# The last block of each MLP: another order of products, a scaled sum in DRAM, and weight forms made ahead

## The chip, the cores and the metric

The kernel runs on one core of a Trainium2 chip. The metric is the time of one execution on the device in microseconds (us). The engines are TensorE (PE, matrix products, with PEld for its weight loads), VectorE (DVE), ScalarE (ACT), GpSimd (POOL) and SyncE (SP). SP and POOL do little but issue transfers here: SP the plain loads, POOL the transfers that copy or add inside DRAM.

## The reference

A trunk of two layers on 512 tokens of width 1024, in float32:

```python
def hybrid_layer(x, ...):
    h = rmsnorm(x, g_mix)
    z = h @ w_in                       # q, k, v of attention and of retention, gates
    ya = sliding_window_sink_attention(aq, ak, av, sinks) @ w_a
    yb = (retention(rq, rk, rv), normed and gated) @ w_b
    x = x + (sigmoid(ga) * ya + sigmoid(gb) * yb) @ w_out
    h2 = rmsnorm(x, g_mlp)
    return x + jnp.square(jax.nn.relu(h2 @ w_up)) @ w_down     # d_ff = 4096

def reference(x, ...):
    for l in range(2):
        x = hybrid_layer(x, ...)
    return rmsnorm(x, g_final)
```

The change lies in the last line of the layer, the MLP, and in what stands around its end: the first projection of the next layer, and the final norm.

## The kernel before, in words

Every product of float32 matrices is made of three matrix products of rounded parts (hi times hi, hi times lo, lo times hi: lines 322 to 324, in `products`). A weight unit of 128x1024 numbers is loaded to a `raw` tile (five buffers), ACT rounds it to `hi` (line 276), and DVE subtracts to get `lo` (line 277); four `hi` and four `lo` buffers exist. `unit` hands out the next unit and has the splitting kept three units ahead and the loading four more. The list of units, and with it the order of loads and splits, is written out by hand in `unit_order`.

The MLP runs in eight blocks of 512 of the 4096 hidden columns. A block makes 512 hidden columns (two calls of `pair`; in block 0 plain products of `w_up`) and then multiplies them into the sum of the MLP in `down(e)`. Both steps use a scheme for a 2x2 split of the matrices that needs seven products instead of eight. Its seven weight forms are blocks of the weights and sums of blocks. In `down`, the seven are units 0 to 6 of the block: w11, a sum from DRAM, w11 plus that sum, w12, another sum from DRAM, the full sum, and w21. Units 2 and 5 are added on DVE from raw tiles that are kept for it (`add_block`, line 258). The sums from DRAM are made earlier by POOL: `sum_steps` is a generator, and each second call of `pace` during the attention and retention part of a layer issues its next step.

Each product of `down` leaves an accumulator in PSUM (a, b or c, two banks each, one per `m`). The four quarters of the output are (i, j): i is the half of the 1024 columns, j the half of the 512 tokens. In blocks 0 to 6 (class `Adding`) ACT copies each finished accumulator to a temporary (lines 1177 and 1182) and POOL issues a transfer that adds it to `y` in DRAM (line 1187). There are seven temporaries, shared with `pair`.

In block 7 (class `Ending`) SP loads the four quarters of `y` into tiles called `big` (line 1199; six buffers, shared with the hidden columns and the forms). ACT multiplies the loaded sum by a factor per token (line 1210), since the norm before the MLP was left out of its input: the square of that norm's scale comes out as a factor on the sum. In layer 1 the residual x is put into `y` too, divided by the factor (`turn_x`). DVE then adds each accumulator times the factor (lines 1228 and 1229). In layer 0 the quarters are turned back by PE (`turn`, line 1252) and added to x by DVE (line 1258); `scaled_input` makes the operands of the next layer from x (lines 332 and 333, tiles xh and xl), and the next layer's first projection (`group`) begins. One quarter is turned after that projection's first unit (`carry`). In layer 1 the quarters get the final norm: ACT sums squares (line 1234), DVE multiplies by the gain (line 1235), ACT takes the root (line 1239), and ACT scales the eight pieces (line 1243), which SP and ACT store (line 1244).

A planner of the framework orders the instructions of each engine: it runs the program on a timing model, and an engine takes the first instruction in program order that the model has ready. The order on the chip is fixed by that; an engine, and the queue of SP or POOL, then waits at an instruction whose inputs are late even if a later one could run.

## Time and profile before

| | |
|---|---|
| median of 3 runs | 1505.0 us (1504.91 to 1506.18) |
| the profiled execution | 1507.86 us, its span 1505.9 us |
| PE busy | 1472.5 us, 98% |
| DVE busy | 1067.4 us, 71% |
| ACT busy | 945.4 us, 63% |
| POOL busy | 228.8 us, 15% |
| mean granted TensorE clock | 0.994 |
| moved | 284.68 MB, mean 189 GB/s |

All positions are microseconds from the start of the span. Layer 0 ends, and layer 1 begins, near 740. The MLP of layer 0 runs from about 430 to 740, that of layer 1 from about 1160 to 1490. In a timeline row the first number is the start, the second the length; several equal instructions in a row are one row with their count. Matmuls overlap: the length of one is longer than the distance to the next, so their cost is the distance between starts.

### The profile page before, as it was taken

How to read it: one execution, taken by the hardware profiler on the slowest of the kernel's cores; microseconds unless marked ns; L12 is line 12 of the kernel's file. 1: busy time of each engine (PE TensorE's matmuls, PEld its weight loads, DVE VectorE, ACT ScalarE, POOL GpSimd, SP SyncE). 2: the span in 40 equal slices, each digit the busy share in tenths (PEclk: the TensorE clock that was granted, in tenths of full speed). 3: DMA queues.
4: the chain of work that ended last, by engine and by line, in shares of the span. 5: the costliest groups of instructions: out<-in, count | busy, mean ns of one | idle time of the engine just before them, and what ended most of it. 6: DMA issues, size and time to landing. Idle time of an engine off the chain costs nothing.

```text
span 1505.9 us, 21268 instructions
## 1 busy us (share of the span) xinstructions
PE 1472.5 (98%) x7767; PEld 1262.5 (84%) x7767; DVE 1067.4 (71%) x1604; ACT 945.4 (63%) x1586; POOL 228.8 (15%) x325
## 2 busy tenths in 40 slices
PE   9999999999999999999899999999999999999995
PEld 7888888888889899989688888888888888898884
DVE  7877568654677777777977775677447677776767
ACT  7656445533567777778765562546325877777777
POOL 0000211100002222222001011111000222222220
PEclk9999999999999999999999999999999999999998
DMA  7663997665227889999736579886642488989993
GB/s 262 188 170 106 278 272 185 182 182 149 94 81 215 211 213 218 222 212 213 241 116 196 145 197 250 232 206 160 192 128 97 124 216 211 211 214 214 215 225 121
DMA packets 101241, 284.68 MB, mean 189 GB/s; under 512 B 11664, under 2 KB 11792, under 8 KB 97040
## 3 DMA queue, kind: packets, MB, share of 16 engines
q0 software_dynamic: 36992, 109.07, 36.8%
q1 hardware_dynamic: 63424, 172.94, 34.0%
q8 instruction: 61, 1.00, 0.3%
q10 hardware_dynamic: 720, 1.31, 0.2%
q14 instruction: 44, 0.36, 0.1%
HBM read 230.32 MB, written 113.25 MB: 228 GB/s over the span
## 4 chain that ended last, share of the span: by engine, by line
PE 80%; DMA 7%; DVE 6%; ACT 4%; issue 2%; POOL 0%; ACTq 0%; DVEq 0%
PE mm L322 21%; PE mm L323 21%; PE mm L324 21%; DMA raw<-w_down_in 3%; DVE lo L277 2%; PE b L324 2%; DMA y<-y 2%; PE b L322 2%; PE b L323 2%; PE rv L322 2%; PE rv L323 2%; PE rv L324 2%; DMA dm<-decay_in 1%; ACT hi L276 1%; PE score L667 1%
## 5 line engine op out<-in xcount | busy, mean ns | idle before, releaser
L277 DVE TENSOR_TENSOR lo<-raw,hi 128x1024 fp32r<-128x1024 f32 (+1 forms) x367 | 429.1, 1172 | 198.0 <-ACT hi L276 195.8
L276 ACT ACTIVATE hi<-raw 128x1024 fp32r<-128x1024 f32 (+1 forms) x366 | 373.9, 1023 | 305.9 <-PE mm L323 204.8
L322 PE MATMUL mm<-xh,hi 128*128 128x512 f32 (+1 forms) x1008 | 358.4, 359 | 7.7 <-ACT eu L1096 4.5
L323 PE MATMUL mm<-xl,hi 128*128 128x512 f32 (+1 forms) x1008 | 358.1, 357 | 0.0
L324 PE MATMUL mm<-xh,lo 128*128 128x512 f32 (+1 forms) x1008 | 356.2, 357 | 0.0
L324 PE MATMUL mm<-r,lo 128*128 128x256 f32 (+1 forms) x768 | 251.3, 327 | 0.7 <-DVE lo L277 0.7
L323 PE MATMUL mm<-r,hi 128*128 128x256 f32 (+1 forms) x768 | 251.1, 327 | 0.0
L322 PE MATMUL mm<-r,hi 128*128 128x256 f32 (+1 forms) x768 | 251.0, 327 | 0.0
L322 PEld LDWEIGHTS mm<-xh,hi 128*128 128x128 f32 x1008 | 191.6, 190 | 35.6 <-ACT eu L1096 6.2
L323 PEld LDWEIGHTS mm<-xl,hi 128*128 128x128 f32 x1008 | 191.8, 190 | 25.7
L324 PEld LDWEIGHTS mm<-xh,lo 128*128 128x128 f32 x1008 | 191.2, 190 | 25.2
L323 PEld LDWEIGHTS mm<-r,hi 128*128 128x128 f32 x768 | 145.7, 190 | 14.8
L322 PEld LDWEIGHTS mm<-r,hi 128*128 128x128 f32 x768 | 145.7, 190 | 14.6
L324 PEld LDWEIGHTS mm<-r,lo 128*128 128x128 f32 x768 | 145.7, 190 | 13.4 <-DVE lo L277 0.9
L1187 POOL DMA_DIRECT2D y<-y x112 | 98.3, 1206 | 66.2 <-ACT y L1182 65.9
L1187 POOL DMA_DIRECT2D y<-eu x56 | 47.3, 852 | 396.5 <-ACT eu L1177 372.7
L324 PE MATMUL mm<-hi,r 128*128 128x512 f32 x256 | 95.3, 391 | 0.5 <-DVE r L330 0.5
L323 PE MATMUL mm<-lo,r 128*128 128x512 f32 x256 | 95.7, 390 | 0.0
L322 PE MATMUL mm<-hi,r 128*128 128x512 f32 x256 | 91.5, 394 | 0.1
L322 PE MATMUL b<-hi,r 128*128 128x512 f32 x192 | 76.3, 398 | 0.2 <-ACT y L1182 0.2
L324 PE MATMUL b<-hi,r 128*128 128x512 f32 x192 | 73.2, 396 | 3.1 <-DVE r L330 3.1
L323 PE MATMUL b<-lo,r 128*128 128x512 f32 x192 | 75.2, 392 | 0.0
(214 smaller groups left out, 2238.6 us busy)
## 6 DMA issues: line engine op xcount, KB each, us to landing
raw<-w_in_in SPq DMA_DIRECT2D x89, 512.0 KB, 5.5
sums_down<-w_down_in POOLq DMA_DIRECT2D x32, 1024.0 KB, 10.7
y<-y POOLq DMA_DIRECT2D x120, 256.0 KB, 8.6
sums_up<-w_pair_in POOLq DMA_DIRECT2D x56, 512.0 KB, 9.4
raw<-w_down_in SPq DMA_DIRECT2D x48, 512.0 KB, 9.1
raw<-w_pair_in SPq DMA_DIRECT2D x84, 256.0 KB, 4.0
raw<-sums_down SPq DMA_DIRECT2D x32, 512.0 KB, 8.4
raw<-sums_up SPq DMA_DIRECT2D x56, 256.0 KB, 4.9
```

The source lines that it names most:

```text
L276: nc.scalar.activation(hi[:, at], raw[:, at], AF.Copy)
L277: nc.vector.tensor_tensor(lo[:, at], raw[:, at], f32(hi[:, at]), ALU.subtract)
L322: nc.tensor.matmul(ps, ah, bh, start=start and i == 0, stop=False, **more)
L323: nc.tensor.matmul(ps, ah, bl, start=False, stop=False, **more)
L324: nc.tensor.matmul(ps, al, bh, start=False, stop=stop and i == n - 1, **more)
L667: nc.tensor.matmul(ps[:, g * w : (g + 1) * w], q_s[g][:, c, at], part[:, keys], start=i == 0, stop=i == 1)
L1187: nc.gpsimd.dma_start(y[:, 2 * j + m, i * T : (i + 1) * T], t, **how)
```

## The change

- In `down` the fifth and sixth products change places: the full sum's product (into c) comes before the one of the second sum from DRAM (into b), and the evictions follow.
- In block 7 the two forms that DVE added (units 2 and 4 in the new order) come from a new array in DRAM, `sums_last`. Three more POOL steps a layer make it, so `pace` issues at five of nine calls.
- `y` in DRAM is kept scaled: ACT's copies in `Adding` multiply by the factor column, and x enters `y` unscaled. The pass of ACT over the loaded `y` goes.
- `y` is loaded ahead of block 7's two calls of `pair` (`Ending()` is built there): in layer 1 into x, which is dead by then, in layer 0 into a tile `late` (the ninth of the slot tiles, moved to a pool of its own) and two `big` tiles. In layer 0 the early part of quarter (1, 1) is added to the loaded tile by a POOL transfer. All other additions read PSUM on DVE.
- In layer 0 the two quarters of the first column half are turned between the sixth and the seventh product, the two others in `carry`; all squares come in `carry`, and the preparation and finishing of the norm's statistics move one unit later in the next layer's first projection.
- In layer 1 the gain is loaded at the start of the MLP, the dummy square root reads the factor column and so can't run before it, and the final scaling of one half of the columns is done by DVE.

```diff
+        e = N_BLOCK - 1
+        both = sums_last[layer].rearrange("p (a n) -> p a n", a=2)
+        first = sums_down[layer][e][:, UNIT:].unsqueeze(1).broadcast_to([P, 2, UNIT])
+        r11, r12 = (w_down[layer, e][:, a * UNIT : (a + 1) * UNIT] for a in (0, 3))
+        nc.gpsimd.dma_start(both, r11.unsqueeze(1).broadcast_to([P, 2, UNIT]))
+        yield
+        nc.gpsimd.dma_start(both, first, accum_op=ALU.add)
+        yield
+        nc.gpsimd.dma_start(both[:, 1, :], r12, accum_op=ALU.add)
...
-        if steps and pace_count[0] % 2 == 0:
+        if steps and pace_count[0] * 5 // 9 > (pace_count[0] - 1) * 5 // 9:
...
-        if part in (2, 5):
+        if part in (2, 4) and e < N_BLOCK - 1:
             return
...
+            2: (sums_last[layer], 0),
             3: (w_down[layer, e], 3),
-            4: (sums_down[layer][e], 0),
+            4: (sums_last[layer], 1),
+            5: (sums_down[layer][e], 0),
...
-            {0: squares, 1: stats_first} if layer == 0 else {0: carried.pop(), 1: rms_mix.prepare, 2: stats},
+            {0: squares, 1: stats_first} if layer == 0 else {0: carried.pop(), 2: rms_mix.prepare, 3: stats},
...
+        if last:
+            sq = small.tile([P, 3 * NB], F32, tag="sq", name="sq", bufs=1)
+            gain_tile = late_tile(F32)
+            nc.sync.dma_start(gain_tile[:, 0:2, :], g_last)
...
-            nc.scalar.activation(t, ps, AF.Copy, scale=inverse[:, b : b + 1])
+            nc.scalar.activation(t, ps, AF.Copy)
...
             multiply(a, b21, False)
             for m in range(2):
-                sink.put(0, 0, m, a[m], 1)
+                into.put(0, 0, m, a[m], 1)
+            multiply(c, b22, False)
+            for m in range(2):
+                into.put(0, 1, m, c[m], 1)
             multiply(b, u_forms[2], False)
             for m in range(2):
-                sink.put(1, 1, m, b[m], -1, p5[m])
-            multiply(c, b22, False)
-            for m in range(2):
-                sink.put(0, 1, m, c[m], 1, u2[m])
+                into.put(1, 1, m, b[m], -1)
+            into.last_but_one()
             multiply(b, u_forms[3], False)
...
+            def send(self, i, j, m, t, ps, sign, add):
+                block = 2 * j + m
+                nc.scalar.activation(t, ps, AF.Copy, scale=(factor if sign > 0 else negative)[:, block : block + 1])
                 how = {"accum_op": ALU.add} if add else {}
-                nc.gpsimd.dma_start(y[:, 2 * j + m, i * T : (i + 1) * T], t, **how)
+                nc.gpsimd.dma_start(y[:, block, i * T : (i + 1) * T], t, **how)
...
+                for i, j in ((1, 1), (0, 1), (0, 0), (1, 0)):
+                    if last:
+                        two = x[:, 4 * j + 2 * i : 4 * j + 2 * i + 2, :]
+                    elif i == 0:
+                        two = late_box[0][:, 2 * j : 2 * j + 2, :]
+                    else:
+                        two = big("y")
                     nc.sync.dma_start(two, y[:, 2 * j : 2 * j + 2, i * T : (i + 1) * T])
...
-                for i, j in QUADS:
-                    for m in range(2):
-                        v = self.y[i, j, m]
-                        nc.scalar.activation(v, v, AF.Copy, scale=factor[:, 2 * j + m : 2 * j + m + 1])
...
+                    nc.vector.tensor_scalar(v, v, total, None, ALU.mult)
+                    nc.sync.dma_start(out[:, block, T:], v)
+                    v = self.y[0, j, m]
+                    nc.scalar.activation(v, v, AF.Copy, scale=total)
+                    nc.scalar.dma_start(out[:, block, :T], v)
...
+            def last_but_one(self):
+                if not last:
+                    for half in range(2):
+                        for j in range(2):
+                            self.turn(0, j, half, ps_mm)
+                        for k in (2 * half, 2 * half + 1):
+                            scaled_input(k, g_mix + 2)
...
+            def carry(self):
                 for half in range(2):
+                    for j in (1, 0):
+                        self.turn(1, j, half, ps_aux)
+                    for k in (4 + 2 * half, 5 + 2 * half):
+                        scaled_input(k, g_mix + 2)
+                for k in range(KD):
+                    squared_input(k, g_mix + 2)
+                    nc.sync.dma_start(spill[:, k, :], x[:, k, :])
...
+                    nc.scalar.activation(sq[:, 0:1], factor[:, 0:1], AF.Sqrt)
...
+                into = Ending() if e == N_BLOCK - 1 else Adding(e)
                 pair(0)
                 pair(1)
-            down(e)
+            down(e, into)
```

169 lines of the change are left out of this document (78 added, 91 removed).

## The prediction

> **What bounds the kernel now.** I read the page's busy shares first, then PE's waits, then the table of busy time by stretches, and last the timelines of the two stretches where PE loses most.
>
> ```profile
> span 1505.9 us, 21268 instructions
> ...
> PE 1472.5 (98%) x7767; PEld 1262.5 (84%) x7767; DVE 1067.4 (71%) x1604; ACT 945.4 (63%) x1586; POOL 228.8 (15%) x325
> ```
> ```profile
> PE mm L322 <- ACT eu L1096: 4.5, 7, 1.3
> PE b L324 <- DVE r L330: 3.1, 6, 1.7
> ```
> ```profile
> core 0: us, PE busy (x) PEld busy (x) DVE busy (x) ACT busy (x) POOL busy (x), PEclk, DMA share, GB/s
> 40.00:380.00 340.00, 338.91 (x1597) 283.88 (x1596) 232.91 (x420) 170.32 (x294) 38.34 (x68) 1.00 0.69 189
> 733.00:739.00 6.00, 4.13 (x15) 2.31 (x14) 6.00 (x10) 3.27 (x5) 0.00 (x0) 1.00 0.74 238
> 739.00:753.00 14.00, 8.95 (x40) 7.31 (x41) 13.43 (x21) 7.05 (x12) 0.00 (x0) 0.77 0.61 207
> 767.00:781.00 14.00, 14.00 (x64) 11.58 (x63) 11.73 (x13) 9.90 (x13) 0.00 (x0) 1.00 0.30 94
> ```
> ```profile
> 1490.33 0.39 PE L324 MATMUL b<-hi,r 128*128 128x512 f32 x1
> ```
>
> The first fence is the span and the engines' shares, the second two rows of PE's waits (total, count, longest), the third stretches of time with each engine's busy time, the fourth PE's last matmul (start, length). PE is the bound; the change alters none of its products, so only its gaps can move the time. The waits are small all over; PE loses most in two places, both of which the change rebuilds: the passage from layer 0 to layer 1 (733 to 753), and the end, where it stands idle for the last 15 of 1505.9 us. In the passage DVE is busy 6.00 of 6 and 13.43 of 14 us: DVE holds PE there.
>
> **The passage.** 733 to 753 holds 15 + 40 PE instructions; 28 are transposes.
>
> ```profile
> 736.67 0.50 PE L324 MATMUL b<-hi,r 128*128 128x512 f32 x1 [1.66 <-DVE r L330]
> 739.13 2.40 PE L1252 MATMUL turn<-ident,y 128*128 128x128 f32 x20 [0.34 <-DVE y L1229]
> 743.97 0.66 PE L1252 MATMUL turn<-ident,y 128*128 128x128 f32 x4 [2.44 <-DVE x L1258]
> 747.11 2.08 PE L322 MATMUL mm<-xh,hi 128*128 128x512 f32 x4 [2.49 <-ACT xh L332]
> 750.26 0.63 PE L324 MATMUL mm<-xh,lo 128*128 128x512 f32 x1
> 750.69 0.63 PE L323 MATMUL mm<-xl,hi 128*128 128x512 f32 x1
> ```
> ```profile
> 711.00:743.00 32.00, 29.77 (x39) 1.00 0.81 266
> ```
> ```profile
> L1228 DVE SCALAR_TENSOR_TENSOR y<-eu,columns,y 128x512 f32<-128x512 f32 x4 | 2.8, 746 | 0.8 <-ACT y L1210 0.8
> L258 DVE TENSOR_TENSOR raw<-raw 128x1024 f32<-128x1024 f32 x2 | 2.4, 1222 | 0.0
> ```
> ```profile
> 743.23 3.67 DVE L1258 TENSOR_TENSOR x<-x,turn 128x512 f32<-128x512 f32 x6
> ```
>
> The fences are PE's timeline, DVE alone in 711 to 743, two of DVE's groups there, and its additions to x. Full-rate matmuls come at 14/64 = 0.22 us, transposes at 2.40/20 = 0.12 us. So the 20 us hold 27 x 0.22 + 28 x 0.12 = 9.3 us of PE work, and 10.7 are lost: in waits, and at 750 in matmuls 0.43 us apart.
>
> The change takes from DVE two weight additions (2.4), two of the four L1228 (1.4; a POOL transfer does them) and the wait for the scaling (0.8). It puts the four additions to x that the first operands need ahead of the last quarter's, so two of the six L1258 (3.67/6 each, 1.2) and that quarter's two additions to y (the same kind of step as L1228, 1.5) come later. The first xh comes 7.3 us earlier, at about 739.0 instead of 746.3. PE arrives there at about 738.6: its seventh product ends 1.7 earlier, and 16 transposes (1.9) now stand ahead of it. With so short a wait I let the clock hold, which saves 12 x (0.43 - 0.22) = 2.5. Eight more transposes (1.0) go into the next projection. Sum: 7.3 + 2.5 - 1.0 = 8.8; I take 8, since squares crowd DVE later. Bounds: 2.4 (the removed additions alone) and 10.7 (all that is lost).
>
> By the Trainium skill, page "TensorE: Matmul & The Clock Gate", section "What's actually happening", the clock halves after an idle window of about 3.4 us. This passage shows it halved after two gaps of only 2.44 and 2.49 us with transposes between, and the same page's section "Part 4: PE-mode transpose" says these don't count as busy in the same way. By that rule 1.9 us of transposes and a wait of 2 us would still halve it; the sum would then be about 6 instead of 8.
>
> What is late next is the statistics, one unit later in the projection.
>
> ```profile
> 769.16 0.39 PE L464 MATMUL ssq<-sl,ones 128*128 128x512 f32 x1
> ```
> ```profile
> 770.46 3.35 DVE L466 RECIPROCAL rstd<-rstd 128x512 f32<-128x512 f32 x1 [0.78 <-ACT rstd L465]
> 773.85 1.22 DVE L507 TENSOR_TENSOR tab<-rawtab,rstd 128x1024 f32<-128x1024 f32 x1
> ```
>
> The two sums of squares would follow the last product of `group`, whose four accumulators wait for them; only one of five banks is free, which covers one `chunk`, 24 x 0.22 = 5.3 us. From the second sum's start to the tables took 775.07 - 769.16 = 5.9, and an addition-sized DVE step (0.7) frees the first bank: 6.6. A wait of 1.3; I take 1.5, between 0 and the whole 5.3.
>
> **The end.**
>
> ```profile
> 1494.05 2.49 DVE L1235 TENSOR_TENSOR y<-y,gain 128x512 f32<-128x512 f32 x4
> 1495.63 0.85 ACT L1239 ACTIVATE sq<-sq 128x1 f32<-128x1 f32 x4
> 1496.65 1.94 ACT L1243 ACTIVATE y<-y,sq 128x512 f32<-128x512 f32 x3 [0.17 <-DVE sq L1240]
> 1500.33 1.32 ACT L1243 ACTIVATE y<-y,sq 128x512 f32<-128x512 f32 x2
> ```
> ```profile
> 1465.00:1497.00 32.00, 30.83 (x50) 0.95 0.34 119
> ```
> ```profile
> L568 DVE TENSOR_SCALAR r<-klo,x 128x512 fp32r<-128x512 f32 x4 | 1.8, 481 | 0.0
> ```
>
> The fences: the end's timeline, DVE alone in the last stretch, and a scaling on DVE of the size that the change adds. PE ends at 1490.7, but DVE (30.83 of 32 us) works on to 1496.5; only then come the eight scalings on ACT, to 1501.65. The change takes from DVE two weight additions (2.4) and a wait for the scaling (0.8 in layer 0; I take 0.5), and adds two scalings of the finished half ahead of the end (2 x 0.48). DVE is through at 1494.6; a root and a reciprocal (0.4, since four roots take 0.85), and two scalings on each engine (1.33 on ACT, the longer) end it at 1496.4: 5.3 earlier. Bounds: 2 (DVE's own removal less some crowding) and 7.9: if the earlier loads let the additions keep up, PE's end at 1490.7, plus an addition (0.75), a square (0.6, as ACT's copies of that size below), root and reciprocal (0.4) and scalings (1.33), gives 1493.8.
>
> **The other parts.**
>
> ```profile
> L332 ACT ACTIVATE r<-rv,rcol 128x512 fp32r<-128x512 f32 x16 | 10.9, 689 | 8.6 <-PE rv L324 8.6
> L329 ACT ACTIVATE r<-pT 128x512 fp32r<-128x512 f32 x24 | 13.8, 591 | 12.6 <-PE pT L632 12.6
> L276 ACT ACTIVATE hi<-raw 128x1024 fp32r<-128x1024 f32 x333 | 352.8, 1060 | 292.8 <-PE mm L323 196.9 <-issue 45.0 <-PE mm L324 21.4
> ```
> ```profile
> y<-y POOLq DMA_DIRECT2D x120, 256.0 KB, 8.6
> raw<-w_down_in SPq DMA_DIRECT2D x48, 512.0 KB, 9.1
> sums_down<-w_down_in POOLq DMA_DIRECT2D x32, 1024.0 KB, 10.7
> ```
> ```profile
> 1454.72 0.33 SPq L251 DMA_DIRECT2D raw<-sums_down  x1
> 1463.15 19.50 SPq L1199 DMA_DIRECT2D y<-y  x4
> ```
> ```profile
> 1446.18 7.13 POOL L1187 DMA_DIRECT2D y<-y  x8 [5.03 <-ACT y L1182]
> ```
> ```profile
> DMA to landing us min/median/max: 2.6/7.1/16.1
> ```
> ```profile
> 1466.71 1.06 ACT L276 ACTIVATE hi<-raw 128x1024 fp32r<-128x1024 f32 x1
> ```
>
> These are, in turn: groups of ACT by form; issues of transfers with the median time to landing; SP's and POOL's timelines in block 7 of layer 1; the landing times of the additions issued at L1187; and ACT's rounding of unit 1 of that block.
>
> Copies with a factor column: 14 blocks x 12 copies, each longer by 689 - 591 = 98 ns (the same copy from PSUM with and without a column), 16.5 us of ACT in all. ACT waited 292.8 us ahead of the `hi` copies, so most is free; PE does wait for ACT at L1096 (4.5 in 7). Cost 1.5, between 0 and 16.5, near the lower since that wait shows the usual cover.
>
> The swapped products: both last products use b, so each bank's eviction (0.69) must fit into the other bank's six matmuls (1.3). It fits unless ACT is at a `hi` copy (1.06). Cost 0.5; bounds -1.4 (what is left of the b waits outside the passage, 3.1 - 1.7) and 14 x 0.69 = 9.7.
>
> The early loads of `y` stand on SP ahead of later weight loads of block 7, and wait there for block 6's additions to land; the weights queued behind wait too, then share the transfers with 2 MB of `y` and two more forms of 0.5 MB. PE has the split units and a few loads as cover. Cost 2 for both layers; bounds 0 (what earlier loads gain stands in the bounds of the end) and 18 (first rival).
>
> `sums_last`: three more POOL transfers a layer, about 10.7 us each, in stretches where PE lost 1.1 of 340 us at a transfer share of 0.69. The weights' cover is their loading seven units ahead. Cost 0; without it the loss there could double, so 0 to 2. The mark copies of `pace` and POOL's queue hold nothing PE needs at that time. The gain load and the early loading into x and `late` cost nothing, since nothing else uses these tiles then: the MLP hides them. In layer 0 two `y` tiles now hold two of six `big` buffers through both pairs, which use four; without that margin a pair's first copy would wait for the block before, so 0 again. The POOL transfer that adds the early part of quarter (1, 1) lands after 8.6 us; DVE's addition to it follows four products later (4 x 12 x 0.22 = 10.6), so it is hidden by 2 us; a later landing would hold DVE's queue and with it the turns, and stands in the passage rival. Earlier eviction of c is part of the swap's lower bound.
>
> **The sum.** -8 + 1.5 - 5.3 + 1.5 + 0.5 + 2 + 0 = -7.8. The profiled execution took 1507.86 (1505.9 span, 2.0 around it), 2.9 above the median; the differences carry over to the median: 1505.0 - 7.8 = 1497.2.
>
> **The rivals.** *SP held (slower).* The last of block 6's additions was issued by 1453.3 and such a transfer can take 16.1 us, so SP, blocked from about 1453, is free at 1469 instead of issuing unit 1 at 1454.7. That is 14.3 us late. The cover: the load would have landed at 1463.8 (9.1), rounding began at 1466.71, 2.9 later, and PE holds split units for some 2.5 (a unit is 12 matmuls, 2.6). So 9 us of stall a layer, 18 instead of 2: 1513.2. It decides from a stall of 4.9 us a layer, where all gain is gone. For it: additions are already late, ACT stands for them ahead of L1096. Against: the planner may place the y loads behind the weights, as it did at 1463, and 8.6 is the median.
>
> *ACT in the way (slower).* All 98 ns of the 168 copies fall on PE: 16.5 instead of 1.5, 1512.2. For it: PE's most frequent wait is on ACT; against: ACT's own waits.
>
> *The passage stays.* DVE's backlog moves into the projection and the clock halves again: its lower bound 2.4 instead of 8, 1502.8, a change that does little of what it says. For it: squares, additions and splits of all eight pieces fall into four units. Against: those units last 24 x 0.22 x 4 = 21 us, more than DVE needs.
>
> *All of it works.* No cost from SP, ACT, b and statistics, and the end bound by PE: 7.8 + 5.5 + 2.6 = 15.9, 1489.1.
>
> **Chances and range.** My forecast 0.52 (own range 1491 to 1501), all works 0.12, passage stays 0.14, SP held 0.13, ACT 0.09. The runs before spread by 1.3 us; 0.2% (3.0 us) is about what can be told. Faster: 0.52 + 0.12 + 0.03 of the passage's = 0.67; same 0.11; slower 0.22. The range 1487 to 1510 leaves out the upper halves of the two slower ones.
>
> **What would show it.** Right: the waits of `turn` and `xh` gone and the clock full near 740; the last scaling near 1494 in a span near 1498; no wait over 1 us on `lo` in block 7. Wrong: SP waiting many us at the y loads with PE waits on L277 or L330 behind it, a longer L1096 wait, or half-rate matmuls at the projection's start.

## The result, and the profile after

The changed kernel takes 1519.1 us (median of 4 runs, 1514.7 to 1521.2) against 1505.4 for the kernel before on the same chip: a ratio of 1.0087, interval 1.0062 to 1.0111. It is slower by about 14 us, where 8 us less were forecast. The profiled execution took 1520.3 us.

First the page of the changed kernel (span, PE's share), then its waits of PE (what PE waited for: total us, times, longest):

```profile
span 1518.4 us, 21303 instructions
...
PE 1477.2 (97%) x7767; PEld 1271.5 (84%) x7767; DVE 1059.8 (70%) x1602; ACT 945.6 (62%) x1560; POOL 239.6 (16%) x337
```
```profile
PE mm L347 <- ACT eu L1129: 11.6, 7, 5.3
PE ret L347 <- DVE s L851: 8.4, 2, 4.5
PE mm L347 <- DVE rot L541: 3.6, 1, 3.6
PE b L347 <- DVE y L1248: 1.4, 1, 1.4
PE mm L347 <- ACT xh L357: 1.2, 2, 0.8
```

PE's work is the same 7767 matmuls. Three waits are new or longer: for `eu`, an accumulator's copy that ACT makes in a pair (4.5 us in all before, 11.6 now), for `s`, the masked scores of the retention (1.6 before, 8.4 now), and for `rot`, the rotated keys of layer 1. The waits that the prediction aimed at, `turn` and `xh`, are gone or short. The table by stretches (columns as in the prediction) shows where the new waits lie and that the granted clock falls behind each:

```profile
250.00:290.00 40.00, 35.52 (x164) 30.08 (x163) 21.47 (x36) 15.70 (x26) 4.83 (x9) 0.91 0.74 192
715.00:730.00 15.00, 11.44 (x66) 10.55 (x65) 7.71 (x11) 9.36 (x16) 0.96 (x1) 0.77 1.00 386
730.00:751.00 21.00, 19.30 (x95) 15.75 (x93) 20.37 (x28) 11.62 (x18) 1.75 (x2) 1.00 0.75 208
770.00:795.00 25.00, 21.44 (x88) 17.25 (x87) 19.67 (x25) 14.91 (x23) 0.00 (x0) 0.93 0.31 93
1465.00:1490.00 25.00, 19.70 (x126) 18.56 (x126) 13.32 (x18) 14.30 (x26) 1.04 (x2) 0.86 0.91 293
```

The passage (730 to 751) now runs at the full clock. The retention (250 to 290), the last block of each layer (715 to 730, 1465 to 1490) and the first projection of layer 1 (770 to 795) don't. The timelines of the changed kernel show the three places; in layer 0's last block these are two rows of SP, one of ACT and one of PE (start, length; in brackets the idle time before and what ended it):

```profile
705.63 3.53 SPq L1233 DMA_DIRECT2D late<-y  x2
709.26 0.42 SPq L255 DMA_DIRECT2D raw<-w_pair_in  x1
...
718.20 0.63 ACT L301 ACTIVATE hi<-raw 128x512 fp32r<-128x512 f32 x1 [4.46 <-DMA raw<-w_pair_in]
...
722.12 0.58 PE L347 MATMUL mm<-xh,hi 128*128 128x256 f32 x1 [3.56 <-ACT eu L1129]
```

SP issues two loads of `y`, then the last part of the last pair's weights; ACT starts on that part 8.9 us later, after 4.46 us of standing for it, and PE stands 3.56. Is the load slow, or was it issued late? The first pair of rows is the same load and the one ahead of it before the change, the third row is the one ahead of it now; below each stands the time that the load took to land.

```profile
697.62 0.33 SPq L229 DMA_DIRECT2D raw<-sums_up  x1
699.49 0.33 SPq L231 DMA_DIRECT2D raw<-w_pair_in  x1
DMA to landing us min/median/max: 7.9/7.9/7.9
```
```profile
702.49 0.33 SPq L253 DMA_DIRECT2D raw<-sums_up  x1
DMA to landing us min/median/max: 8.8/8.8/8.8
```

It was issued late: 6.8 us behind the load ahead of it instead of 1.9. In layer 1 it is 6.4 instead of 1.9, with 9.0 us to land instead of 8.9. SP's waits say for what SP stood, in layer 0 (690 to 740) and in layer 1 (1440 to 1500):

```profile
SPq L1233 <- DMA y<-y: 10.0, 5, 3.2
```
```profile
SPq L1233 <- DMA y<-y: 11.2, 4, 3.1
```

In the retention DVE waits for a tile of the decay, `dm`, before (first) and after the change:

```profile
268.72 1.16 DVE L826 TENSOR_TENSOR s<-ret,dm 128x512 f32<-128x512 f32 x2 [5.21 <-DMA dm<-decay_in]
```
```profile
274.62 1.48 DVE L851 TENSOR_TENSOR s<-ret,dm 128x512 f32<-128x512 f32 x3 [10.54 <-DMA dm<-decay_in]
```

Last, the passage and the end of the changed kernel: the first matmul of layer 1's projection, PE's last matmul, and the last scaling.

```profile
751.46 1.20 PE L347 MATMUL mm<-xh,hi 128*128 128x512 f32 x4 [0.76 <-ACT xh L357]
...
1506.24 0.39 PE L349 MATMUL b<-hi,r 128*128 128x512 f32 x1
...
1512.51 0.72 ACT L1267 ACTIVATE x<-x,sq 128x512 f32<-128x512 f32 x1 [0.42 <-DVE x L1264]
```

Some landmarks, read from the timelines, give the loss by place. A block's mark is the start of ACT's first copy of b<-mm.

| mark | before | after | later by |
|---|---|---|---|
| layer 0, block 0 | 439.5 | 444.6 | 5.1 |
| layer 0, block 6 | 677.7 | 681.8 | 4.1 |
| layer 1, block 0 | 1185.4 | 1198.9 | 13.5 |
| layer 1, block 6 | 1429.4 | 1439.9 | 10.6 |
| PE's last matmul | 1490.3 | 1506.2 | 15.9 |
| end of the span | 1505.9 | 1518.4 | 12.5 |

Each layer loses ahead of its MLP and in its last block; blocks 0 to 6, the passage and the stretch behind the last matmul gain.

### The profile page after: what moved, and what is told of

Read it like the earlier page. It is cut to its first block, busy times and chain, and to the rows that moved or that the text cites. A ratio compares the mean times of both kernels' runs of the same rounds, so it can differ in the third digit from the quotient of the medians.

```text
span 1518.4 us, 21303 instructions
## 1 busy us (share of the span) xinstructions
PE 1477.2 (97%) x7767; PEld 1271.5 (84%) x7767; DVE 1059.8 (70%) x1602; ACT 945.6 (62%) x1560; POOL 239.6 (16%) x337
## 4 chain that ended last, share of the span: by engine, by line
PE 72%; DMA 11%; issue 7%; DVE 5%; ACT 3%; POOL 1%; SPq 0%; DVEq 0%; ACTq 0%; POOLq 0%
PE mm L347 19%; PE mm L348 19%; PE mm L349 19%; DMA raw<-w_pair_in 3%; DMA raw<-w_down_in 2%; DMA y<-y 2%; DMA dm<-decay_in 2%; DVE lo L302 2%; PE rv L347 2%; DMA y<-eu 2%; PE rv L349 2%; PE rv L348 2%; ACT hi L301 1%; PE b L347 1%; PE b L348 1%
## 5 line engine op out<-in xcount | busy, mean ns | idle before, releaser
L347 PE MATMUL mm<-xh,hi 128*128 128x512 f32 (+1 forms) x1008 | 360.0, 360 | 16.5 <-ACT eu L1129 11.6
L347 PE MATMUL mm<-r,hi 128*128 128x256 f32 (+1 forms) x736 | 239.1, 325 | 0.5 <-ACT mm L1127 0.5
L348 PE MATMUL mm<-r,hi 128*128 128x256 f32 (+1 forms) x736 | 239.3, 325 | 0.0
L349 PE MATMUL mm<-r,lo 128*128 128x256 f32 (+1 forms) x736 | 239.2, 325 | 0.0
L347 PEld LDWEIGHTS mm<-xh,hi 128*128 128x128 f32 x1008 | 192.4, 191 | 45.2 <-ACT eu L1129 13.5
L347 PEld LDWEIGHTS mm<-r,hi 128*128 128x128 f32 x736 | 140.5, 191 | 13.8 <-ACT mm L1127 0.7
L348 PEld LDWEIGHTS mm<-r,hi 128*128 128x128 f32 x736 | 140.4, 191 | 13.3
L349 PEld LDWEIGHTS mm<-r,lo 128*128 128x128 f32 x736 | 140.3, 191 | 11.3
L261 DVE TENSOR_TENSOR raw<-raw 128x512 f32<-128x512 f32 x56 | 38.5, 687 | 66.1 <-DMA raw<-sums_up 53.8
L347 PE MATMUL b<-hi,r 128*128 128x512 f32 x192 | 75.3, 392 | 1.9 <-DVE y L1248 1.4
## 6 DMA issues: line engine op xcount, KB each, us to landing
sums_down<-w_down_in POOLq DMA_DIRECT2D x32, 1024.0 KB, 11.3
```

Source lines behind the costliest of these rows:

```text
L261: nc.vector.tensor_tensor(raws[i][:, at], last[:, LEFT], last[:, RIGHT], ALU.add)
L347: nc.tensor.matmul(ps, ah, bh, start=start and i == 0, stop=False, **more)
L348: nc.tensor.matmul(ps, ah, bl, start=False, stop=False, **more)
L349: nc.tensor.matmul(ps, al, bh, start=False, stop=stop and i == n - 1, **more)
```

## The experiments

Three theories stood at first: the loads of `y` make the weights late (A1), the denser pace of POOL's steps makes the decay late (A2), the later statistics make PE wait for the rotation (A3). Times are medians; "before" is the kernel before on the same chip. The groups e1 to e4, e5 to e7, e8 to e12 and e13 to e15 come from four chips, on which the kernel before took 1506.9, 1505.6, 1506.7 (1506.6 beside e12) and 1505.2 us. Where a difference across groups carries a reading, it is also given with each run set against its own "before".

| run | us | ratio to before | interval |
|---|---|---|---|
| e1_loads_late | 1519.2 | 1.0085 | 1.0056 to 1.0114 |
| e2_pace_half | 1509.8 | 1.0030 | 1.0013 to 1.0046 |
| e3_stats_early | 1517.5 | 1.0081 | 1.0055 to 1.0108 |
| e4_all_three | 1506.1 | 0.9994 | 0.9981 to 1.0006 |
| e5_y_behind | 1496.7 | 0.9940 | 0.9917 to 0.9963 |
| e6_y_pool | 1500.5 | 0.9977 | 0.9960 to 0.9994 |
| e7_y_behind_dve | 1501.8 | 0.9969 | 0.9957 to 0.9981 |
| e8_extra_copy | 1506.0 | 0.9989 | 0.9968 to 1.0010 |
| e9_stats_late | 1503.9 | 0.9981 | 0.9968 to 0.9994 |
| e10_order_before | 1500.2 | 0.9962 | 0.9947 to 0.9976 |
| e11_turns_late | 1494.9 | 0.9918 | 0.9890 to 0.9945 |
| e12_dense | 1503.8 | 0.9980 | 0.9969 to 0.9991 |
| e13_copy_elsewhere | 1502.5 | 0.9983 | 0.9970 to 0.9996 |
| e14_one_step | 1498.3 | 0.9955 | 0.9943 to 0.9967 |
| e15_again | 1495.7 | 0.9948 | 0.9932 to 0.9964 |

**e1: the loads of `y` behind the pairs, in the program.**

```diff
-                into = Ending() if e == N_BLOCK - 1 else Adding(e)
                 pair(0)
                 pair(1)
+                into = Ending() if e == N_BLOCK - 1 else Adding(e)
```

> The changed kernel with one edit: in the last block the four loads of `y` are issued behind the two pair units again, as before the change; they still fall into the tiles that are free. Theory A (SP is held): SP waits for the sum in DRAM (11.2 us in the last block of layer 1, 10.0 in that of layer 0), the weight loads queued behind these waits come late and PE stands 5.3 and 3.6 us for the splits, with its clock halved behind each. It expects both PE waits for `eu` above 3 us gone, the ground lost over the two blocks (8.6 us from block 6 to block 7 in layer 0, 6.0 in layer 1) mostly back, so 1519.1 - 12 to 1519.1 - 14.6: 1504 to 1507 us. Rival B (the transfers themselves): the weights are late because all forms of the last block are now read from DRAM and the DMA engines are full; then SP's waits become short but the splits stay late and the time stays within 3 us of 1519.

1519.2 us: no change. SP's and PE's timelines of this run say why:

```profile
704.76 3.55 SPq L1233 DMA_DIRECT2D late<-y  x2
708.40 0.64 SPq L255 DMA_DIRECT2D raw<-w_pair_in  x1
```
```profile
720.67 0.58 PE L347 MATMUL mm<-xh,hi 128*128 128x256 f32 x1 [5.12 <-ACT eu L1129]
```

The two loads stand ahead of the weights as before the edit; only the other two moved behind them (to 729.5), and that changed nothing. The planner orders a queue by when its model has an instruction ready; in the model `y` must have been ready first. The run said nothing on A1; it only showed that the edit had not done what it said.

**e2: the first 20 steps of POOL at the old pace.**

```diff
-        if steps and pace_count[0] * 5 // 9 > (pace_count[0] - 1) * 5 // 9:
+        if steps and (pace_count[0] % 2 == 0 or pace_count[0] % 48 > 40):
```

> The changed kernel with one edit: the first 20 steps of POOL's sums are issued at every second call of the pace, as before the change, and the steps of `sums_last` follow at the last calls of the layer. Theory A (density): five steps in nine calls push the 1 MB transfers of `sums_down` into the stretch in which the retention reads its decay, so the third decay tile lands 16.0 us after its issue instead of 13.0 and DVE, then PE, wait for it (10.54 us on DVE instead of 5.21; PE 8.4 us for `s` instead of 1.6). It expects PE's wait for `s` back under 2 us, block 0 of each layer 4 to 5 us earlier, 1509 to 1511 us in all. Rival B (the new data): it is the 5 MB more that `sums_last` moves in each layer that fills the engines; then the late steps move the trouble elsewhere and the time stays at 1516 to 1521.

1509.8 us, 9.2 less, as A2 expected, though `sums_last` is still made. PE's wait for the scores:

```profile
PE ret L347 <- DVE s L851: 1.9, 2, 1.3
```

8.4 us have become 1.9, and layer 0's block 0 stands at 438.0 instead of 444.6. The last six steps, the three new ones among them, are issued call by call at the end of the layer and cost nothing ahead of that block; what costs is that the denser pace moved the older steps of the layer.

**e3: the statistics one unit earlier.**

```diff
-            {0: squares, 1: stats_first} if layer == 0 else {0: carried.pop(), 2: rms_mix.prepare, 3: stats},
+            {0: squares, 1: stats_first} if layer == 0 else {0: carried.pop(), 1: rms_mix.prepare, 2: stats},
```

> The changed kernel with one edit: the statistics of layer 1's mix stand one unit earlier again, where they were before the change. Theory A (the statistics): the wait of PE for `rot` (3.6 us, once, at 784 us) with the lower clock behind it (0.91 in that stretch) comes from the later statistics; it expects that wait gone and 1514 to 1516 us. Rival B (a new wait): the carried turns come at the first unit, so the sums of squares are not ready one unit later; PE then waits 2 to 5 us for the accumulated squares, and the time is 1517 to 1521. Rival C: the rotation is late because DVE is behind with other work of that stretch; the wait for `rot` stays.

1517.5 us; with four runs on each side that spread by 5 to 7 us, that is no difference. The wait for `rot` was halved, not gone:

```profile
PE mm L347 <- DVE rot L541: 1.8, 1, 1.8
```

**e4: the three edits together.**

```diff
-                into = Ending() if e == N_BLOCK - 1 else Adding(e)
                 pair(0)
                 pair(1)
+                into = Ending() if e == N_BLOCK - 1 else Adding(e)
...
-        if steps and pace_count[0] * 5 // 9 > (pace_count[0] - 1) * 5 // 9:
+        if steps and (pace_count[0] % 2 == 0 or pace_count[0] % 48 > 40):
...
-            {0: squares, 1: stats_first} if layer == 0 else {0: carried.pop(), 2: rms_mix.prepare, 3: stats},
+            {0: squares, 1: stats_first} if layer == 0 else {0: carried.pop(), 1: rms_mix.prepare, 2: stats},
```

> The changed kernel with the three edits together: loads of `y` behind the pair units, the first 20 steps at every second call, the statistics one unit earlier. Theory A (three separate causes that add): 1519 less 13, 9 and 4.5, which is 1491 to 1494 us and 11 to 14 below the kernel before; what is left of the change is the regained passage (8 us), the shorter tail (3.4) and the faster adding blocks (3.4). Rival B (one cause behind all, or each loss uncovers another): less than two thirds of the three single gains, 1500 us or more.

1506.1 us: level with the kernel before, and rival B of that run by its number. The waits of PE show what was left:

```profile
PE mm L347 <- ACT eu L1129: 13.4, 6, 5.3
```

The wait for `eu` is not smaller, since the first edit left two loads of `y` ahead of the weights. A1 was still to be tried. The run takes 3.7 us less than e2, and since the moved loads changed nothing in e1, that goes to the earlier statistics.

**e5: the loads of `y` queued behind the last weight load.** Pace and statistics as in e4; the four loads carry an ordering edge to the load of unit 6 of block 7.

```diff
+    last_load = {}
...
-        nc.sync.dma_start(raw, source[:, at * UNIT : (at + 1) * UNIT])
+        load = nc.sync.dma_start(raw, source[:, at * UNIT : (at + 1) * UNIT])
+        if e == N_BLOCK - 1 and part == 6:
+            last_load[layer] = load.ins
...
             multiply(a, b11)
+            if into is None:
+                with tc.issue_after(last_load[layer]):
+                    into = Ending()
...
-                into = Ending() if e == N_BLOCK - 1 else Adding(e)
+                into = None if e == N_BLOCK - 1 else Adding(e)
```

> The kernel with the first 20 steps at every second call and the earlier statistics, and with the four loads of `y` queued on SP behind the last weight load of block 7 (the run before had moved them in the program only, and the planner put two of them ahead of the weight loads again). Theory A (the 2 MB of `y` stand ahead of the weights, held or not): PE's waits of 5.3 us for `eu` in block 7 of both layers go, with the half clock behind each (5 us at 0.50 cost some 2.5 us): 1506.1 - 2 x 5.3 - 2 x 2 = 1491 to 1494 us. Rival B (the 1 MB more of ready forms in block 7 is what fills the transfer engines): the last part of the last pair still comes more than 3 us late and the time stays above 1500. Rival C (`y` is now late): the waits move to DVE's additions and PE waits 2 us or more for an accumulator before the sixth product; 1496 to 1502.

1496.7 us: 9.4 less than e4 (8.1 with each against its own "before"), and 0.6% below the kernel before. In SP's timeline the weights now come first, 3.0 us behind the load ahead of them, and in PE's the wait of layer 0's last block has shrunk from 5.3 to 1.2; that of layer 1's is gone:

```profile
699.22 0.33 SPq L255 DMA_DIRECT2D raw<-w_pair_in  x1
...
715.41 0.89 SPq L1240 DMA_DIRECT2D late<-y  x2
```
```profile
711.28 0.38 PE L351 MATMUL mm<-xh,hi 128*128 128x256 f32 x1 [1.19 <-ACT eu L1133]
```

The late `y` has a price of its own. The POOL transfer into quarter (1, 1) lands late, DVE stands for it with the turns queued behind, and the passage runs below the full clock again in this run (DVE's timeline, then the stretch 740 to 750):

```profile
733.72 0.75 DVE L1255 SCALAR_TENSOR_TENSOR y<-b,columns,y 128x512 f32<-128x512 f32 x1 [1.88 <-DMA y<-eu]
```
```profile
740.00:750.00 10.00, 8.75 (x36) 7.33 (x37) 10.00 (x17) 8.21 (x15) 0.00 (x0) 0.83 0.73 262
```

From block 7's mark to the first copy of `rot` it takes 48.7 us here, 42.6 in the changed kernel, 45.2 in e1 and 53.9 before. In e15, the same kernel with its instructions in the same order, the clock of 740 to 750 is 1.00 and the passage takes 47.8, only 0.9 less.

**e6: `y` where the change has it, but issued by POOL,** with pace and statistics as in e4.

```diff
-                    nc.sync.dma_start(two, y[:, 2 * j : 2 * j + 2, i * T : (i + 1) * T])
+                    nc.gpsimd.dma_start(two, y[:, 2 * j : 2 * j + 2, i * T : (i + 1) * T])
```

> The same base (first 20 steps at every second call, earlier statistics), with the loads of `y` where the change has them in time, but issued by POOL instead of SP, so that SP never waits for the sum in DRAM. Theory A1 (SP is held): the weights behind are issued in time, the last part of the last pair is at hand, the waits of 5.3 us go: 1491 to 1495 us. Theory A2 (the transfers themselves are in the way): the 2 MB of `y` still move between 705 and 720, ahead of or beside the weights; PE still waits 3 to 5 us for `eu` and the time is 1502 to 1507.

1500.5 us, between the two expectations. PE's longest wait for `eu`:

```profile
712.75 0.39 PE L347 MATMUL mm<-xh,hi 128*128 128x256 f32 x1 [1.80 <-ACT eu L1129]
```

SP issues the last pair's weights 3.0 and 2.6 us behind the load ahead of them, as in e5, and they land after 7.4 and 6.0 us, though the first two loads of `y` still move in the same stretch. PE's waits for `eu` in the two last blocks, 10.6 us together in e4, are 2.9 here and 1.2 in e5: most of them go when SP no longer stands still. What the bytes alone cost is small there: ACT waits 2.1 us in layer 0 for the next weight unit, against 0.6 in e5. The times divide less clearly. The step from e4 is 5.7 us, but 4.4 with each run against its own "before"; the 3.8 us left to e5, on the same chip, also hold a wait of 1.8 for `rot` that e5 hasn't.

**e7: the two ready forms of block 7 added on DVE again,** with `y` behind the weights, as e5. The three steps of `sums_last` are taken out too.

```diff
-        if part in (2, 4) and e < N_BLOCK - 1:
+        if part in (2, 4):
             raws[i] = raws.pop(i - 2)
             nc.vector.tensor_tensor(raws[i], raws[i], raws.pop(i - 1), ALU.add)
```

> As the run with `y` behind the last weight load, and with the two ready forms of block 7 added on DVE again (no `sums_last`, so 2 MB in each layer less to make and 1 MB less to load). If the ready forms are worth something, DVE is late in block 7 with the splits and this run is 1 to 4 us slower than that one; if their transfers cost something, it is 1 to 4 us faster; if both are hidden, within 1 us.

1501.8 us, 5.1 more than e5, so the run as a whole favours the ready forms. That they gain by the four additions of 1.2 us that they spare DVE is not shown: of the 3.7 us between the two traces, 3.2 lie in blocks 0 to 6, whose forms are the same in both, and 2.2 from block 6 of layer 1 on.

**e8: a copy of 1.5 MB that nobody reads, in the stretch of the decay,** on e5.

```diff
             with tc.issue_after(ins.ins):
+                if pace_count[0] % 48 == 36:
+                    n = pace_count[0] // 48
+                    nc.gpsimd.dma_start(scratch[n], w_down[n, 0][:, : 3 * UNIT])
```

> A control for the pace: the run with `y` behind the last weight load (1496.7 us), with one copy of 1.5 MB inside DRAM added to POOL's queue in each layer near 248 and 988 us, between the second and third tile of the decay; nothing reads what it writes, and no other order changes. Theory A (transfers of the sums in that stretch make the decay late): the decay tile issued at 258 lands some 15 us after its issue instead of 9, DVE waits near 10 us for it instead of 4 to 5, PE's waits for `s` rise from 2.6 to 7 us or more, and the time rises by 6 to 10 us, to 1503 to 1507. Rival B (the denser pace costs by its copies on POOL, or by when the later sums are done): the decay is not moved by it and the time stays within 2 us of 1496.7.

1506.0 us, 9.3 more than e5 and 11.1 more than e11, the same kernel as e5 on this chip. DVE's wait for the decay, 4.4 us in e5, nearly doubles:

```profile
271.74 1.49 DVE L859 TENSOR_TENSOR s<-ret,dm 128x512 f32<-128x512 f32 x3 [8.25 <-DMA dm<-decay_in]
```

But block 0 of layer 0 is only 3.6 us later (441.2 against 437.6), and 5.3 us are lost in blocks 0 to 6 of layer 1, where no copy runs. PE, DVE and ACT also run some instructions near the late decay in another order than in e5, which the expectation had ruled out. The total fitted the theory, its place did not; e13 takes this up.

**e9: the statistics late again,** on e5.

```diff
-            {0: squares, 1: stats_first} if layer == 0 else {0: carried.pop(), 1: rms_mix.prepare, 2: stats},
+            {0: squares, 1: stats_first} if layer == 0 else {0: carried.pop(), 2: rms_mix.prepare, 3: stats},
```

> The run with `y` behind the last weight load, with the statistics of layer 1 again one unit later, as in the change. If they cost what the prediction put on them, 1498.2 us (0 to 5 more than 1496.7) with a wait of PE for `rot` near 784 us of 2 us or more; if they are free, 1496 to 1497.5 and no such wait.

1503.9 us: 7.2 more than e5, and 9.0 more than the same kernel on this chip (e11). The chain behind the sums of squares, in the timeline:

```profile
768.09 0.39 PE L493 MATMUL ssq<-sl,ones 128*128 128x512 f32 x1
...
770.21 0.69 ACT L494 ACTIVATE rstd<-ssq,x 128x512 f32<-128x512 f32 x1
770.93 3.35 DVE L495 RECIPROCAL rstd<-rstd 128x512 f32<-128x512 f32 x1 [0.77 <-ACT rstd L494]
774.32 1.23 DVE L536 TENSOR_TENSOR tab<-rawtab,rstd 128x1024 f32<-128x1024 f32 x1
775.46 1.22 DVE L306 TENSOR_TENSOR lo<-raw,hi 128x1024 fp32r<-128x1024 f32 x1
776.60 0.69 DVE L545 TENSOR_TENSOR rot<-mm,tab 128x512 f32<-128x512 f32 x1
...
777.43 0.47 PE L351 MATMUL mm<-xh,hi 128*128 128x512 f32 x1 [3.51 <-DVE rot L545]
...
779.48 0.63 PE L351 MATMUL mm<-xh,hi 128*128 128x512 f32 x1
779.90 0.63 PE L352 MATMUL mm<-xl,hi 128*128 128x512 f32 x1
```

From the second sum to PE's next matmul it takes 9.3 us: ACT takes the root 2.1 us after the sum, and DVE subtracts a weight (775.46, 1.2 us) between the table and the rotation. A few us of matmuls behind the wait come 0.43 us apart (last two rows) instead of 0.22. From block 7 of layer 0 to block 0 of layer 1 the trace is 3.9 us longer than in e5, 3.3 than in e11 and 5.5 than in e15; the rest of the 7 to 9 isn't found at one place.

**e10: the products of blocks 0 to 6 in the order of before,** on e5; block 7 keeps the new order.

```diff
-            multiply(c, b22, False)
-            for m in range(2):
-                into.put(0, 1, m, c[m], 1)
-            multiply(b, u_forms[2], False)
-            for m in range(2):
-                into.put(1, 1, m, b[m], -1)
+            for quarter in (0, 1) if e == N_BLOCK - 1 else (1, 0):
+                if quarter == 0:
+                    multiply(c, b22, False)
+                    for m in range(2):
+                        into.put(0, 1, m, c[m], 1)
+                else:
+                    multiply(b, u_forms[2], False)
+                    for m in range(2):
+                        into.put(1, 1, m, b[m], -1)
```

The units of these blocks are loaded and added in the old order too (lines left out here).

> The run with `y` behind the last weight load, with the products of blocks 0 to 6 in the order of before (the full sum before the second sum of DRAM; block 7 keeps the new order). If the new order costs the 0.5 us of the prediction, 1496; if it is what made blocks 0 to 6 of layer 1 shorter (241.0 us from block 0 to block 6 against 244.0 before), 1499 to 1501 us, and these stretches are longer by 1 to 3 us; if neither, within 1 us.

1500.2 us: 3.5 more than e5, 5.3 more than e11. From block 0 to block 6 it takes 239.4 us in layer 0 and 244.7 in layer 1, against 237.9 and 242.7 in e5. PE's wait for the low parts that DVE makes is back:

```profile
PE b L354 <- DVE r L360: 1.7, 9, 0.4
```

The stretches are 3.5 us longer in all than in e5 (3.3 to 4.4 over e5, e11 and e15), so the new order is a gain here. Its size is less sure than these figures look, since in e8 and e13 the same stretch of layer 1 grew by 3 to 5 us for no reason that was found. Against the kernel before (238.2 and 244.0) the same two stretches are 1.2 and 0.7 longer; what is known to differ there is the copies with a factor.

**e11: the turns behind the seventh product,** on e5.

```diff
-            into.last_but_one()
             multiply(b, u_forms[3], False)
             for m in range(2):
                 into.put(1, 0, m, b[m], -1)
+            into.last_but_one()
             into.end()
```

> The run with `y` behind the last weight load, with the turns of the first column half in layer 0 behind the seventh product instead of between the sixth and the seventh. Theory (the passage is paid by PE waiting for x and then running at half clock): PE waits 2 us or more for the turns and 2 to 3 us for `xh` again, the clock falls below 0.8 near 740 to 750, and the time is 1502 to 1506 us. Rival (the passage is short because `y` is scaled, not because of the turns): less than 2 us more than 1496.7.

1494.9 us. The order of the instructions on all five engines is that of e5: the planner had put the turns where it wanted them both times. This is a second measurement of e5, no test of the turns.

**e12: five of nine calls, with the other two causes removed.** The changed kernel with the loads of e5 and the statistics of e3, so e5 with

```diff
-        if steps and (pace_count[0] % 2 == 0 or pace_count[0] % 48 > 40):
+        if steps and pace_count[0] * 5 // 9 > (pace_count[0] - 1) * 5 // 9:
```

> The changed kernel with two edits: `y` behind the last weight load, and the earlier statistics; the pace stays at five of nine calls. With the changed kernel (1519.1), the half pace alone (1509.8) and all three edits (1496.7 and 1494.9) it closes a square of two causes. If the pace costs the same with and without the other two (9 us), the time is 1504 to 1506, with a wait of DVE near 10 us for the decay in layer 0 and 8 to 9 in layer 1, and the first block of layer 0 near 444 instead of 438 us; if the early `y` and the later statistics were what the denser pace collided with, the time is 1496 to 1499.

1503.8 us, with DVE's wait for the decay long again:

```profile
272.77 1.49 DVE L855 TENSOR_TENSOR s<-ret,dm 128x512 f32<-128x512 f32 x3 [9.62 <-DMA dm<-decay_in]
```

The square closes: the pace costs 9.2 us in the changed kernel and 7.1 to 8.9 here; the other two together cost 15.3 at the dense pace and 13.2 to 14.9 at the half one. The pace and the other two, taken together, add. Within the two it depends on the order: the later statistics cost 1.6 us in e3 (inside the spread), 3.7 from e2 to e4 and 7.2 to 9.0 in e9.

**e13: the copy of e8 four calls earlier,** near 228 and 969 us.

```diff
-                if pace_count[0] % 48 == 36:
+                if pace_count[0] % 48 == 32:
```

> The same added copy of 1.5 MB a layer as in the control, but four calls of the pace earlier, near 228 and 969 us, where the transfer engines have shares of 0.36 to 0.88 and no decay is on its way. Theory A (the place of the bytes): DVE's wait for the decay at 266 us stays at 4 to 5 us, and the time is within 2 us of the repeat without a copy (1495 to 1498). Rival B (bytes as such, or what the array in DRAM moves elsewhere): the time rises as in the control, to 1501 to 1506, again with the loss in the MLP of layer 1.

1502.5 us, 3.5 less than e8 (1.9 with each against its own "before"), and block 0 of layer 0 is back at 437.6, 3.6 us earlier:

```profile
266.21 1.16 DVE L859 TENSOR_TENSOR s<-ret,dm 128x512 f32<-128x512 f32 x2 [4.24 <-DMA dm<-decay_in]
```

Both expectations were half right. DVE's wait and the mark show what the copy's place costs, and it lies where theory A has it. But 6.8 us above e15 remain, 3.0 of them in blocks 0 to 6 of layer 1 and 2.4 behind, though the instructions of PE, DVE, ACT and SP are in the order of e5. Both runs with the additional array lose there. Whether the array shifts others in DRAM wasn't tried, and this loss stays open.

**e14: one step of layer 0 later,** on e12: no step at call 36 (near 249 us), one more at call 39 (near 275).

```diff
-        if steps and pace_count[0] * 5 // 9 > (pace_count[0] - 1) * 5 // 9:
+        dense = pace_count[0] * 5 // 9 > (pace_count[0] - 1) * 5 // 9
+        if steps and (dense and pace_count[0] % 48 != 36 or pace_count[0] % 48 == 39):
```

> The kernel at five of nine calls, `y` behind the last weight load and the earlier statistics (1503.8), with one single step of layer 0 moved from the call near 249 us to one near 275. Theory A: with 0.5 MB less in the stretch the decay lands earlier, DVE waits 4 to 7 us for it instead of 9.6, the first block of layer 0 starts near 439 to 440 instead of 442.2 us, and the time is 1500 to 1502. Rival B (the density over the whole layer): no change, 1503 to 1505, the first block at 442 us.

1498.3 us, 5.5 less than e12 (4.0 with each against its own "before"), and block 0 of layer 0 stands at 436.9 instead of 442.2, 5.3 earlier:

```profile
265.06 1.15 DVE L856 TENSOR_TENSOR s<-ret,dm 128x512 f32<-128x512 f32 x2 [3.14 <-DMA dm<-decay_in]
```

More moved than the 0.5 MB that the expectation names. A step is a copy and an addition, and the steps behind it shift as well: the copy of 0.5 MB at 248.6 goes to 262.6, an addition of 1 MB from 259.1 to 263.1, and the next step from 262.4 to 273.0, while the decay's load is issued near 257.8 in both. This shift is worth 4 to 5.5 us and is the cleanest test of A2 in layer 0. The other 2.6 us up to e15, on the same chip, fit layer 1, where DVE still waits 8.6 us for the decay.

**e15: e5 once more,** with no edit.

> The kernel with `y` behind the last weight load, half pace and earlier statistics once more, as the base of the two runs beside it: 1494 to 1498 us, a ratio to the kernel before of 0.990 to 0.995.

1495.7 us. The kernel of e5, e11 and e15 has been measured on three chips, at ratios of 0.9940, 0.9918 and 0.9948: 8 to 12 us below the kernel before, and the fastest of all.

## Why the prediction was wrong

By its own steps, with what each term measured:

| term | forecast, bounds | measured | by |
|---|---|---|---|
| passage | -8, -10.7 to -2.4 | -11.3; -8.7; -5.2 to -6.1 | block 7's mark to the first `rot` copy against before: changed kernel; e1; e5, e11 and e15 |
| statistics | +1.5, 0 to 5.3 | +3.7; +7.2 to +9.0 (3.3 to 3.9 in their stretch) | e2 against e4; e9 against e5 and e11 |
| end | -5.3, -7.9 to -2 | -3.4 | last matmul to the end: 15.6, then 12.2 |
| copies with a factor | +1.5, 0 to 16.5 | +1.9 | blocks 0 to 6, e10 against before |
| swapped products | +0.5, -1.4 to 9.7 | -3.5 to -5.3 | e10 against e5 and e11 |
| early loads of `y` | +2, 0 to 18 | +9.4 (+8.1 against each "before") | e4 against e5 |
| `sums_last` and pace | 0, 0 to 2 | +7.1 to +9.2 | e2, e12 |

Along one path, from the changed kernel over e2 and e4 to e5, the costs come off as 9.2, 3.7 and 9.4 us. What the other terms give at its end (passage -5.2 to -6.1, end, copies, swap) is 10 to 13 us of gain. Together that is 9 to 12 of the 14 us; with runs that spread by 6 us the rest can't be put anywhere.

**The step that failed outright is the pace,** the term of `sums_last`. The prediction priced the three new steps (0, at most 2), from "stretches where PE lost 1.1 of 340 us at a transfer share of 0.69". Two things were wrong in it. The edit of `pace` moves the 23 older steps as well, and these are what hurt (e2 keeps the new ones, and its block 0 of layer 0 stands at 438.0, against 439.5 before). And the mean hid the stretch that counts. In the kernel before, that stretch reads:

```profile
250.00:260.00 10.00, 10.00 (x48) 8.37 (x47) 10.00 (x18) 6.37 (x10) 1.78 (x4) 1.00 0.96 231
260.00:270.00 10.00, 8.91 (x42) 7.12 (x41) 2.20 (x6) 1.56 (x2) 1.54 (x3) 1.00 1.03 289
```

The share of the transfer engines (last but one) is 0.96 and 1.03: there was no room for one more step, and DVE waited 5.2 us for the decay already. Its load landed 9.2 us after its issue; in the changed kernel it took 16.0. "The weights' cover" was named, but the decay isn't a weight; it is loaded into a single buffer with nothing ahead.

**The early loads were the rival *SP held*.** Its mechanism came true: SP stood 10 and 11 us for the sum in DRAM, the last pair's weights were issued 4.9 and 4.5 us later behind the load ahead of them than before, and PE stood 3.6 and 5.3 us in the two layers, about the 4.9 from which it was to decide. Two of the prediction's own signs of being wrong are these: SP's wait at the loads and the longer wait for `eu`. Its price (9 us a layer) was too high, the forecast's 2 for both too low; 9.4 were measured. What spoke against it, that the planner may place the loads behind the weights, was a guess: no view of the profile before could show the order that the planner would choose. That SP's standing still is the larger part, and not the 2 MB ahead of the weights, is shown by PE's waits for `eu` in e4, e6 and e5 (10.6, 2.9 and 1.2 us); how the 9.4 us of time divide isn't settled.

**The statistics were mis-sized.** The cover of one `chunk` was right (24 matmuls, 5.4 us in e9). The chain was taken as 5.9 + 0.7 = 6.6 us, as if ACT and DVE were free for it; 9.3 were measured in e9, with a root that comes 2.1 us after the sum and a weight subtraction in between. The kernel before has such a subtraction there too (774.99, with the rotation at 776.12), which the sum left out. Behind the wait comes the clock, which the sum left out too. By the Trainium skill, page "TensorE: Matmul & The Clock Gate", section "What's actually happening", an idle window of about 3.4 us halves the clock; this wait of 3.51 us agrees, with matmuls 0.43 us apart behind it. Not all runs do. In e6 the granted clock (behind the counts) is 0.50 after a wait of only 1.80 us, with the clock at 1.00 and PE busy for 6.95 of the 7 us ahead of 711:

```profile
714.00:717.00 3.00, 3.00 (x12) 2.61 (x12) 2.91 (x6) 3.00 (x7) 0.46 (x1) 0.50 1.03 414
```

So no least wait for the fall of the clock can be taken from these runs.

**Right, by mechanism:** the passage, in the form that the change gave it (clock 1.00 from 730 to 751, the `turn` wait gone and the `xh` wait short). Its size is partly luck. In the changed kernel it gains 11.3 us, more than the upper bound, but block 7's mark stands 48.4 us behind block 6's there (39.8 before), and DVE may catch up while PE stands; with that loss removed the gain is 5.2 to 6.1. Whether the earlier `y` or PE's standing made the difference isn't separated. The copies with a factor came out near their size. The end did by its sign and within its bounds. By the rule of the Trainium skill (the same page and section) that the prediction weighed for the passage, the clock would halve again and the gain be 6 us instead of 8. That did not happen in the changed kernel. In e5 it did: PE's waits between transposes are 1.30, 0.98 and 1.02 us, the clock is 0.83, and the gain is 5.2. In e15 the same instructions keep the clock at 1.00, and the gain is still only 6.1.

**Right in the sum, for the wrong kernel:** with `y` behind the weights, the old pace for the first 20 steps and the statistics where they were, the parts that were meant to gain give 8 to 12 us. That this meets the forecast of 8 is luck in part: the swap, forecast as a cost, is among them; why it gains more than the 1.4 us of its lower bound is not settled beyond the wait of 1.7 us for DVE's low parts.

## What to carry to other kernels

Price the queue before the bytes: for each transfer that moves, list what stands behind it on its queue, and read the transfer share of the 20 us where it lands, not of the stage. A denser pace moves every step, the old ones too. And where a planner orders the queues, an edit in the program is only a wish: look at the order in the trace, and pin it by an edge, before a run is taken for a test.

## What the runs showed of the hardware

A load of 256 KB issued behind two loads of 512 KB on the same queue landed after 8.8 us, while the engines moved 309 GB/s at a share of 1.08 (709.3 to 718.2 of the changed kernel). The same load with no such loads ahead took 7.9 and 8.9 us in the kernel before, so it was late by its issue and not by its landing. One step of POOL fewer near 249 us, with the transfers behind it 4 to 14 us later, changed the time by 4 to 5.5 us. And a gap has a tail: in the changed kernel the granted clock fell to 0.50 inside the wait of 3.56 us and was still 0.50 from 722 to 727, with matmuls 0.21 us apart that come 0.12 us apart otherwise, so that the wait cost more than its length.
